# Layer A of a two-layer decoder: the compressed branch's softmax over two query blocks at once

## The chip, the cores and the metric

The kernel runs on one core of a Trainium2 chip. The metric is the device time of one execution in microseconds (us). Each kernel is timed several times and the median is quoted; one further execution is profiled, and its trace gives every row shown here.

## The reference, cut to what matters

A sequence of 512 tokens of width 1024 goes through two layers. Layer A's mixer is a sparse attention with three branches, joined by sigmoid gates, for 12 query heads of width 64 in 3 groups of 4 that share keys and values. The branch that the change touches is the first one:

```python
k_c = rope(rmsnorm(compress(split_heads(k_cmp, G), 0), k_norm[0]), cmp_end)   # 31 blocks of 32 tokens
v_c = compress(split_heads(v_cmp, G), 1)
m_c = cmp_end[None, :] <= t[:, None]
p_c = masked_softmax(jnp.einsum('bgrqd,bgcd->bgrqc', q_b, k_c) * scale, m_c)
o_c = jnp.einsum('bgrqc,bgcd->bgrqd', p_c.astype(v_c.dtype), v_c)
o_c = jnp.where(m_c.any(-1)[:, None], o_c, 0)
...
return g_b[..., 0:1] * o_c + g_b[..., 1:2] * o_s + g_b[..., 2:3] * o_w
```

So every query of every head has a softmax over at most 31 compressed keys, and the first 31 queries, which see none of them, get zero. The other two branches attend to all earlier tokens (with 512 tokens the selection and the window leave nothing out). Beside the mixer runs a small attention over 256 memory tokens; then come an output projection and an MLP, and layer B with a dilated attention, its own memory attention and its MLP.

## The kernel before, in words

**Tiles.** The 512 queries are 4 blocks of 128 (`NB = 4`). The large products are taken as three products of rounded halves (`mm3`, L241 to L247). Weights come by `wdma` (L213 to L216) on SyncE's queue into one of 3 `st` buffers, are split on ScalarE and VectorE (`wsplit`, L235 to L239, the instructions at L237 and L239) and are then free to be overwritten by the next load. Scores of attention go into the PSUM pool `pS` of 3 banks, turned probabilities into `pT` of 2 banks.

**Items and filler.** `attend` (L129) writes layer A's attention as a list of items. An item has a front (scores and softmax) and a back (transposes, and at some items the product with the values), and an item's back is written after the next item's front. After each front and each back a number of filler steps is written, `RA[group]` on average: steps of the projection of the next group (`proj_a`), of the memory keys and values (`mem_kv`), of the memory queries and of the output projection, in the order in which `layer_a` adds them to `work`. The third group's projection and the memory queries wait until all items of group 0 or 1 have had their front (`seen.count(0) == 20`, `seen.count(1) == 20`). The numbers 20 are 16 attention items and 4 compressed ones.

**Order on the engines.** What is written is not yet the order of the engines: the framework (`schedule_with_timeline_sim=True`, L1809) plans each engine's own order beforehand by its planned times. On the chip each engine then keeps to that order.

**The compressed branch.** `compress` (L822) makes the compressed keys `KC` and values `vc`; `vc` is written by a VectorE addition at L905. For each group `cmp_scores` (L935) makes `VCB`, in which the group's 32 compressed values stand four times on different partitions and columns: one clear on GpSimd (L941) and four copies of 32x64 on ScalarE (L943). An item (`front`, L948, and `back`, L973) is one block of 128 queries with the 4 heads of the group:

- 4 matmuls of 64 columns into one `pS` tile (L951);
- on VectorE two additions that read that tile (L956, L957), a maximum (L959), a subtraction (L960), after the exponential on ScalarE (L961) a sum (L963), a reciprocal (L964) and the gate's product (L969; L967 for the first block, with the factor that clears the first 31 queries);
- on GpSimd the product with gate over sum (L970), on TensorE one transpose (L975), and a copy out of PSUM by `evT`.

The tile on which this happens is `s_cs`, from a pool of **two** buffers (`cs=2`, L184): it is taken by L956 and is free again when the transpose L975 has read it. The `pS` bank is free when L957 has read it. `cmp_out` (L980) multiplies `VCB` with the transposed probabilities (L981) at the end of each pair of heads.

`evT` (L678) copies on VectorE (L682) where a running count of all tiles made, `self.n`, can be divided by 3, else on ScalarE (L684). So which engine copies depends on how many tiles have been made before.

Each group has 16 attention items (fronts at L1018 to L1022 for the first two blocks, at L1031 to L1034 for the others, exponentials at L1040, scaling on GpSimd at L676, transposes at L1061 and L1067, product with the values at L1080) and 4 compressed ones. `spread` sets these in after six attention items in group 0 and after one in groups 1 and 2, and from there every second item.

Of the kernel before, what the change touches and what calls it, by code (L numbers as in the profile page):

```python
# [10 lines left out]
BF16 = mybir.dt.bfloat16  # L11
# [36 lines left out]
RA = (1.5, 1.16, 1.46, 1.96)  # L48
# [119 lines left out]
class K:  # L168
# [193 lines left out]
    def setup(self):  # L362
        nc, ins = self.nc, self.ins
        on = self.c("on1", [P, P])
        nc.vector.memset(on, 1.0)
        self.on1 = on[:, 0:1]
        n = self.n
# [47 lines left out]
    def setup2(self):  # L415

        nc = self.nc
        self.x = [None] * KT
        self.idr = self.c("idr", [P, P], F32R)
        nc.vector.tensor_copy(self.idr, self.idf)  # L420
        self.idb, self.cm = [self.c(n, [P, P], BF16) for n in ("idb", "cm")]
        nc.vector.tensor_copy(self.idb, self.idf)
        nc.vector.tensor_copy(self.cm, self.cm0)
        for a, z, g in ((0, NQ, -(HD**-0.5) / KN), (NQ, NK, -1.0 / KN)):
            nc.vector.tensor_scalar(
                out=self.gr[:, a:z], in0=self.gr[:, a:z], scalar1=g, scalar2=None, op0=ALU.mult
            )
# [289 lines left out]
    def layer_a(self):  # L717
# [35 lines left out]
        work.add(self.proj_a(2, xg, st, ga[2]), "g2", lambda: seen.count(0) == 20)  # L753
        work.add(self.mem_q(0, xg, ins["w_am"], e, qm), None, lambda: seen.count(1) == 20)
# [5 lines left out]
        items = spread(L[0], C[0], 6, 1) + spread(L[1], C[1], 1, 1) + spread(L[2], C[2], 1, 1) + M  # L760
# [174 lines left out]
    def cmp_scores(self, g, q4, cmp, gt):  # L935
# [6 lines left out]
        for q in range(4):  # L942
            nc.scalar.activation(  # L943
                VCB[32 * q : 32 * q + 32, q // 2, (q % 2) * HD : (q % 2 + 1) * HD], vc[32 * g : 32 * g + 32, :], AF.Copy
            )
        pcT = self.t("x", [P, S])

        def front(i):  # L948
            Sc = self.ps(self.pS, [P, 4, 2, 32])
            for h in range(4):  # L950
                nc.tensor.matmul(  # L951
                    Sc[:, h].rearrange("p t c -> p (t c)"), q4[h // 2][:, h % 2, i * P : (i + 1) * P],
                    KC[:, g].rearrange("p t c -> p (t c)"), start=True, stop=True,
                )
            s = self.t("cs", [P, 4, 32])
            nc.vector.tensor_tensor(out=s, in0=Sc[:, :, 0], in1=bcast(self.ccm[:, i, :], 1, 4), op=ALU.add)  # L956
            nc.vector.tensor_tensor(out=s, in0=Sc[:, :, 1], in1=s, op=ALU.add)  # L957
            m = self.t("c1", [P, 4])
            nc.vector.tensor_reduce(out=m, in_=s, axis=AX.X, op=ALU.max)  # L959
            nc.vector.tensor_tensor(out=s, in0=s, in1=bcast(m, 2, 32), op=ALU.subtract)  # L960
            nc.scalar.activation(s, s, AF.Exp)  # L961
            z = self.t("c2", [P, 4])
            nc.vector.tensor_reduce(out=z, in_=s, axis=AX.X, op=ALU.add)  # L963
            nc.vector.reciprocal(out=z, in_=z)  # L964
            gc = gt[:, i, :].rearrange("p (h b) -> p h b", b=3)[:, 4 * g : 4 * g + 4, 0]
            if i == 0:
# [19 lines left out]
    def attn_a(self, g, ga, gt, cmp, out):  # L986
# [61 lines left out]
        def back(pr, half, hp, ii, p):  # L1048
# [43 lines left out]
            [Item(cfront, cback, (i,), g, "cmp") for i in range(NB)],  # L1092
# [721 lines left out]
```

## Time and profile before

| | us |
|---|---|
| median of 3 runs | 1267.33 |
| lowest and highest run | 1264.51, 1268.48 |
| the profiled execution, its own time | 1264.88 |
| its span from the first to the last instruction | 1263.1 |

TensorE's granted clock was 0.999 of full speed over the span. A row of the trace names the line, the engine (PE is TensorE's matmul, PEld its weight load, DVE VectorE, ACT ScalarE, POOL GpSimd, SPq SyncE's queue), the operation, the tile written and the tiles read, and the shapes. Idle time is put down to what ended it, the releaser. The attention of layer A lies between 97 and 300 us of the span; the last of the 12 compressed items ends at 244 us.

### The profile page before, as it was taken

The page shows a single profiled execution, that of the slowest core. Times are in us where ns is not written, and L with a number is a line of the kernel's source. Part 1 is how long each engine was busy: PE and PEld are TensorE (multiplying, and loading weights), DVE is VectorE, ACT ScalarE, POOL GpSimd, SP SyncE. Part 2 cuts the span into 40 slices and gives each one's busy share as a digit, 9 for nine tenths or more (in the row PEclk, how much of TensorE's full clock was granted, in tenths as well). Part 3 has the DMA queues.
Part 4 walks back from the last instruction along what each step waited for, and adds up shares of the span by engine and source line. Part 5 has one row for each costly group of instructions (what it writes and reads, how often), then busy time and mean ns, then how long its engine had stood idle before and what let it go on. Part 6 is the DMA issues. An engine that isn't in the chain of part 4 may idle for free.

```text
span 1263.1 us, 18587 instructions
## 1 busy us (share of the span) xinstructions
PE 1232.9 (98%) x6445; PEld 1013.6 (80%) x6445; DVE 971.0 (77%) x1793; ACT 762.9 (60%) x1763; POOL 416.2 (33%) x449
## 2 busy tenths in 40 slices
PE   9998999999999999999999999999999999999998
PEld 8776677677788888888888899888688888888887
DVE  6968878864679678686799968886678868678687
ACT  6656767774476464553656567887776455455462
POOL 0666465543133133250332612222313225033231
PEclk9999999999999999999999999999999999999999
DMA  8311311023532525326235332212242532624423
GB/s 312 112 63 62 108 35 60 9 68 105 162 101 84 167 84 173 120 92 184 99 104 173 108 117 59 68 35 80 86 141 83 172 117 96 183 99 140 142 85 117
DMA packets 52717, 139.10 MB, mean 110 GB/s; under 512 B 5680, under 2 KB 14896, under 8 KB 52624
## 3 DMA queue, kind: packets, MB, share of 16 engines
q1 hardware_dynamic: 51568, 135.50, 34.1%
q0 software_dynamic: 480, 1.38, 0.3%
q8 instruction: 51, 0.84, 0.3%
q10 hardware_dynamic: 576, 1.05, 0.2%
q14 instruction: 42, 0.34, 0.1%
HBM read 132.66 MB, written 5.24 MB: 109 GB/s over the span
## 4 chain that ended last, share of the span: by engine, by line
PE 87%; DVE 6%; ACT 3%; DMA 2%; issue 1%; POOL 1%; SPq 0%; POOLq 0%; DVEq 0%; ACTq 0%
PE s_ps L247 27%; PE s_ps L244 14%; PE s_acc L247 13%; PE s_pt L247 8%; PE s_acc L244 7%; PE s_pt L244 4%; PE s_po L1080 2%; PE s_acc L845 1%; PE s_ps L1031 1%; PE s_pt L1067 1%; PE s_ps L1541 1%; PE s_pt L701 1%; DVE s_w L263 1%; ACT s_w L237 1%; DMA s_st<-in_w_ag_dram 1%
## 5 line engine op out<-in xcount | busy, mean ns | idle before, releaser
L247 PE MATMUL s_ps<-s_act,s_w 128*128 128x512 f32 x1184 | 366.1, 390 | 0.0
L239 DVE TENSOR_TENSOR s_w<-s_st,s_w 128x1024 fp32r<-128x1024 f32 (+4 forms) x161 | 189.1, 1177 | 133.6 <-ACT s_w L237 133.4
L247 PEld LDWEIGHTS s_ps<-s_act,s_w 128*128 128x128 f32 x1184 | 221.7, 188 | 45.7 <-DVE s_act L285 0.4
L237 ACT ACTIVATE s_w<-s_st 128x1024 fp32r<-128x1024 f32 (+4 forms) x182 | 165.7, 918 | 143.2 <-PE s_pt L247 44.5
L244 PE MATMUL s_ps<-s_act,s_w 128*128 128x512 f32 x592 | 231.4, 393 | 3.1 <-DVE s_x L817 1.7
L247 PE MATMUL s_acc<-s_w,s_act 128*128 128x512 f32 (+2 forms) x608 | 169.5, 359 | 0.5 <-DVE s_w L263 0.5
L244 PEld LDWEIGHTS s_ps<-s_act,s_w 128*128 128x128 f32 x592 | 110.9, 188 | 28.4 <-ACT s_act L282 3.2
L247 PEld LDWEIGHTS s_acc<-s_w,s_act 128*128 128x128 f32 x608 | 109.1, 191 | 11.2 <-DVE s_w L263 0.7
L1131 POOL TENSOR_TENSOR s_x<-s_qki,s_st 128x512 f32<-128x512 f32 x16 | 25.3, 1582 | 270.8 <-DMA s_st<-in_w_db_dram 204.9
L244 PE MATMUL s_acc<-s_w,s_act 128*128 128x512 f32 (+2 forms) x304 | 111.2, 371 | 3.4 <-ACT s_w L237 3.4
L1131 POOL TENSOR_TENSOR s_x<-s_x,s_st 128x512 f32<-128x512 f32 x32 | 73.9, 2337 | 102.7 <-DVE s_w L239 102.7
L676 POOL TENSOR_SCALAR s_p<-s_p,s_cr 128x256 f32<-128x256 f32 (+3 forms) x128 | 69.3, 555 | 72.3 <-DVE s_cr L1043 35.2
L247 PE MATMUL s_pt<-s_w,s_act 128*128 128x512 f32 x288 | 86.7, 390 | 0.0
L237 ACT ACTIVATE s_w<-s_x 128x512 fp32r<-128x512 f32 x96 | 56.9, 625 | 48.4 <-POOL s_x L1131 32.2
L239 DVE TENSOR_TENSOR s_w<-s_x,s_w 128x512 fp32r<-128x512 f32 x96 | 68.8, 737 | 10.8 <-ACT s_w L237 10.7
L247 PE MATMUL s_ps<-s_w,s_qk 128*128 128x512 f32 x256 | 76.5, 389 | 0.0
L247 PE MATMUL s_acc<-s_w,s_qk 128*128 128x512 f32 x256 | 76.3, 390 | 0.0
L282 ACT ACTIVATE s_qk<-s_p 128x256 fp32r<-128x256 f32 (+1 forms) x96 | 46.9, 489 | 47.2 <-DVE s_p L1259 44.9
L285 DVE TENSOR_TENSOR s_qk<-s_p,s_qk 128x256 fp32r<-128x256 f32 (+1 forms) x96 | 71.8, 758 | 1.5 <-ACT s_qk L282 0.2
L244 PEld LDWEIGHTS s_acc<-s_w,s_act 128*128 128x128 f32 x304 | 57.8, 191 | 9.1 <-ACT s_w L237 3.9
L1253 ACT ACTIVATE s_p<-s_ps 128x512 f32<-128x512 f32 x64 | 37.8, 590 | 44.5 <-PE s_ps L247 43.9
L247 PEld LDWEIGHTS s_pt<-s_w,s_act 128*128 128x128 f32 x288 | 53.9, 188 | 11.2
(335 smaller groups left out, 2728.1 us busy)
## 6 DMA issues: line engine op xcount, KB each, us to landing
s_st<-in_w_db_dram SPq DMA_DIRECT2D x80, 512.0 KB, 3.6
s_st<-in_w_up_dram SPq DMA_DIRECT2D x64, 512.0 KB, 3.7
s_st<-in_w_bq_dram SPq DMA_DIRECT2D x16, 384.0 KB, 3.2
s_st<-in_w_ag_dram SPq DMA_DIRECT2D x11, 512.0 KB, 4.2
s_act<-in_w_c_dram SPq DMA_DIRECT2D x8, 512.0 KB, 5.7
s_st<-in_w_mem_dram SPq DMA_DIRECT2D x8, 512.0 KB, 3.5
s_st<-in_w_ao_dram SPq DMA_DIRECT2D x16, 256.0 KB, 2.8
s_tq<-in_w_db_dram SPq DMA_DIRECT2D x16, 256.0 KB, 3.0
```

The source lines that it names most:

```text
L237: self.high = nc.scalar.activation(w[:, 0], st, AF.Copy)
L239: self.low = e.tensor_tensor(out=w[:, 1], in0=st, in1=w[:, 0], op=ALU.subtract)
L244: mm(ps, lh[0], rh[0], start=start, stop=False, skip_group_check=again)
L247: self.last = mm(ps, lh[i], rh[j], start=False, stop=stop and i != wr, skip_group_check=again)
L263: nc.vector.scalar_tensor_tensor(out=dst[:, 1], in0=src, scalar=g, in1=dst[:, 0], op0=ALU.mult, op1=ALU.subtract),
L282: nc.scalar.activation(dst[:, 0], src, AF.Copy)
L285: nc.vector.tensor_tensor(out=dst[:, 1], in0=src, in1=dst[:, 0], op=ALU.subtract)
L676: self.nc.gpsimd.tensor_scalar(out=p, in0=p, scalar1=c, scalar2=1.0, op0=ALU.mult, op1=ALU.mult)
L701: nc.tensor.transpose(pt[:, h, :].bitcast(F32R), kpair(qi[:, j + h]), self.idr)
L1080: nc.tensor.matmul(O[x * 64 : x * 64 + 64, q0 + o : q0 + 256], v[:, j, br, :], st[x][br][:, j, o:256], start=half == 0 and br == 1 and j = ...
L1131: (e or self.nc.gpsimd).tensor_tensor(out=o, in0=x, in1=b[:, i * 512 : (i + 1) * 512], op=ALU.add)
L1253: nc.scalar.activation(u, ps, AF.Relu)
```

## The change

1. A compressed item takes **two** query blocks: 8 score matmuls into one tile of 512 columns, one chain of VectorE operations of 256 elements (an extra small one for the first pair of a group, in place of the fused gate product), one exponential, one GpSimd product, two transposes into one tile and one copy. There are 2 items in a group, 6 in all, for 4 and 12.
2. `VCB` is filled by four transfers on SyncE's queue for each group, not by four ScalarE copies.
3. The items stand further apart: in group 0 after six attention items and again after four more, in groups 1 and 2 after one and again after three more. The counts 20 become 18, and group 2's share of filler rises from 1.46 to 1.65 steps.
4. The `cs` buffers grow from 512 to 1024 bytes per partition. To make room, the matrix of ones for TensorE's first, idle matmuls lives in a `cs` buffer at the start, only one column of ones is kept, and the 16-bit identity is written over the first half of the mask that has just been copied.

```diff
-RA = (1.5, 1.16, 1.46, 1.96)
+RA = (1.5, 1.16, 1.65, 1.96)
...
-        on = self.c("on1", [P, P])
+        n = self.n
+        self.on1 = self.c("on1", [P, 1])
+        on = self.t("cs", [P, P])
         nc.vector.memset(on, 1.0)
-        self.on1 = on[:, 0:1]
-        n = self.n
+        nc.vector.memset(self.on1, 1.0)
...
-        self.idb, self.cm = [self.c(n, [P, P], BF16) for n in ("idb", "cm")]
+        self.cm = self.c("cm", [P, P], BF16)
+        nc.vector.tensor_copy(self.cm, self.cm0)
+        self.idb = self.cm0[:, 0 : P // 2].bitcast(BF16)
         nc.vector.tensor_copy(self.idb, self.idf)
-        nc.vector.tensor_copy(self.cm, self.cm0)
...
-        work.add(self.proj_a(2, xg, st, ga[2]), "g2", lambda: seen.count(0) == 20)
-        work.add(self.mem_q(0, xg, ins["w_am"], e, qm), None, lambda: seen.count(1) == 20)
+        work.add(self.proj_a(2, xg, st, ga[2]), "g2", lambda: seen.count(0) == 18)
+        work.add(self.mem_q(0, xg, ins["w_am"], e, qm), None, lambda: seen.count(1) == 18)
...
-        items = spread(L[0], C[0], 6, 1) + spread(L[1], C[1], 1, 1) + spread(L[2], C[2], 1, 1) + M
+        items = spread(L[0], C[0], 6, 4) + spread(L[1], C[1], 1, 3) + spread(L[2], C[2], 1, 3) + M
...
         for q in range(4):
-            nc.scalar.activation(
-                VCB[32 * q : 32 * q + 32, q // 2, (q % 2) * HD : (q % 2 + 1) * HD], vc[32 * g : 32 * g + 32, :], AF.Copy
+            nc.sync.dma_start(
+                VCB[32 * q : 32 * q + 32, q // 2, (q % 2) * HD : (q % 2 + 1) * HD], vc[32 * g : 32 * g + 32, :]
             )
...
-            Sc = self.ps(self.pS, [P, 4, 2, 32])
-            for h in range(4):
+            Sc = self.ps(self.pS, [P, 2, 4, 2, 32])
+            two = slice(2 * i, 2 * i + 2)
+            for j in range(2):
+                for h in range(4):
...
-            s = self.t("cs", [P, 4, 32])
-            nc.vector.tensor_tensor(out=s, in0=Sc[:, :, 0], in1=bcast(self.ccm[:, i, :], 1, 4), op=ALU.add)
-            nc.vector.tensor_tensor(out=s, in0=Sc[:, :, 1], in1=s, op=ALU.add)
+            s = self.t("cs", [P, 2, 4, 32])
+            nc.vector.tensor_tensor(out=s, in0=Sc[:, :, :, 0], in1=bcast(self.ccm[:, two, :], 2, 4), op=ALU.add)
+            nc.vector.tensor_tensor(out=s, in0=Sc[:, :, :, 1], in1=s, op=ALU.add)
...
+            nc.vector.tensor_tensor(out=z, in0=z, in1=gc, op=ALU.mult)
             if i == 0:
-                nc.vector.scalar_tensor_tensor(out=z, in0=z, scalar=self.zc, in1=gc, op0=ALU.mult, op1=ALU.mult)
-            else:
-                nc.vector.tensor_tensor(out=z, in0=z, in1=gc, op=ALU.mult)
+                nc.vector.tensor_scalar(out=z[:, 0], in0=z[:, 0], scalar1=self.zc, scalar2=None, op0=ALU.mult)
...
-            pt = self.ps(self.pT, [P, P])
-            nc.tensor.transpose(pt, s.rearrange("p h c -> p (h c)"), self.idf)
-            self.evT(pcT[:, i * P : (i + 1) * P], pt)
+            pt = self.ps(self.pT, [P, 2, P])
+            for j in range(2):
+                nc.tensor.transpose(pt[:, j], s[:, j].rearrange("p h c -> p (h c)"), self.idf)
+            self.evT(pcT[:, 2 * i * P : 2 * i * P + 2 * P].rearrange("p (j q) -> p j q", j=2), pt)
...
-            [Item(cfront, cback, (i,), g, "cmp") for i in range(NB)],
+            [Item(cfront, cback, (i,), g, "cmp") for i in range(NB // 2)],
```

## Rows read from the trace of the kernel before

**Rows 1.** The page's first part: busy time of each engine, share of the span and number of instructions.

```profile
PE 1232.9 (98%) x6445; PEld 1013.6 (80%) x6445; DVE 971.0 (77%) x1793; ACT 762.9 (60%) x1763; POOL 416.2 (33%) x449
```

**Rows 2.** Busy time by stretch: the stretch, its length, the busy time and instructions of each engine, the granted clock, the DMA share and GB/s.

```profile
97.00:151.00 54.00, 46.12 (x296) 34.97 (x295) 46.24 (x123) 41.81 (x123) 30.72 (x40) 1.00 0.30 99
151.00:205.00 54.00, 54.00 (x353) 44.22 (x351) 41.62 (x112) 34.49 (x112) 35.44 (x51) 1.00 0.14 40
205.00:258.00 53.00, 48.47 (x356) 33.39 (x355) 41.25 (x120) 38.89 (x122) 25.50 (x45) 1.00 0.08 26
```

**Rows 3.** What TensorE waited for from 97 to 151 us: the waiting matmul, the releaser, us in total, times, the longest.

```profile
PE s_acc L244 <- ACT s_w L237: 2.8, 2, 1.9
PE s_ps L1018 <- ACT s_p L1040: 1.5, 1, 1.5
PE s_ps L951 <- DVE s_cs L957: 1.2, 1, 1.2
...
PE s_ps L1031 <- DVE s_cs L957: 0.6, 1, 0.6
```

**Rows 4.** The same from 205 to 258 us.

```profile
PE s_ps L1031 <- ACT s_p L1040: 1.0, 4, 0.5
...
PE s_ps L1031 <- DVE s_cs L957: 0.3, 1, 0.3
PE s_ps L951 <- ACT s_p L1040: 0.3, 1, 0.3
```

**Rows 5.** The chain of work that ended last, from 108 to 134 us: start, us, what. Six more pieces of L943 lie at the first "...", so the eight copies fill 114.50 to 116.47 us.

```profile
114.50 0.11 ACT s_ki L943
...
116.22 0.25 ACT s_ki L943
...
116.50 1.06 ACT s_w L237
...
117.58 1.24 DVE s_w L239
...
118.84 3.37 DMA s_st<-in_w_mem_dram
...
123.99 4.03 DMA s_st<-in_w_ag_dram
```

**Rows 6.** TensorE in order of time (start, us, what): scores of the third and fourth compressed item of group 0 and the transpose of its first; scores of the third item of group 2 and the transpose of its first.

```profile
110.73 0.61 PE L951 MATMUL s_ps<-KC,s_qk 128*128 128x64 f32 x4
...
115.08 0.61 PE L951 MATMUL s_ps<-KC,s_qk 128*128 128x64 f32 x4
...
121.87 0.27 PE L975 MATMUL s_pt<-c,s_cs 128*128 128x128 f32 x1
...
225.49 0.63 PE L951 MATMUL s_ps<-KC,s_qk 128*128 128x64 f32 x4 [0.28 <-ACT s_p L1040]
...
231.86 0.27 PE L975 MATMUL s_pt<-c,s_cs 128*128 128x128 f32 x1
```

**Rows 7.** VectorE in order of time, in brackets the idle time before and its releaser.

```profile
113.25 0.21 DVE L905 TENSOR_TENSOR s_ab<-s_pt,gr 96x64 f32<-96x64 f32 x1
...
124.47 0.28 DVE L957 TENSOR_TENSOR s_cs<-s_ps,s_cs 128x128 f32<-128x128 f32 x1
...
130.88 0.28 DVE L957 TENSOR_TENSOR s_cs<-s_ps,s_cs 128x128 f32<-128x128 f32 x1
...
148.61 0.28 DVE L956 TENSOR_TENSOR s_cs<-s_ps,c 128x128 f32<-128x128 f32 x1
148.81 0.21 DVE L506 SCALAR_TENSOR_TENSOR s_r<-s_r,ec,s_r 128x4 f32<-128x4 f32 x1
...
200.72 0.41 DVE L574 TENSOR_TENSOR s_tq<-s_acc,gr 128x256 f32<-128x256 f32 x1
201.05 0.15 DVE L507 SCALAR_TENSOR_TENSOR s_r<-s_r,s_r 128x4 f32<-128x4 f32 x1
201.12 0.15 DVE L1042 RECIPROCAL s_cr<-s_su 128x2 f32<-128x2 f32 x1
...
232.17 0.29 DVE L956 TENSOR_TENSOR s_cs<-s_ps,c 128x128 f32<-128x128 f32 x1 [2.17 <-PE s_pt L975]
```

**Rows 8.** Groups of instructions by line and shape, 0 to 400 us: busy us, mean ns of one, the idle time before them and its releasers.

```profile
L943 ACT ACTIVATE s_ki<-s_ab 32x64 f32<-32x64 f32 x12 | 3.0, 253 | 0.1
...
L961 ACT ACTIVATE s_cs<-s_cs 128x128 f32<-128x128 f32 x12 | 3.8, 315 | 3.5 <-DVE s_cs L960 3.1 <-DVE s_c L969 0.3
...
L970 POOL TENSOR_TENSOR s_cs<-s_cs,s_c 128x128 f32<-128x128 f32 x12 | 4.8, 397 | 5.9 <-DVE s_c L969 4.9 <-DVE s_cr L1042 0.8 <-PE s_pt L1067 0.2
...
L682 DVE COPY s_pt<-s_pt 128x384 f32<-128x384 f32 x10 | 5.5, 551 | 3.6 <-PE s_pt L1067 3.6
...
L682 DVE COPY s_pt<-s_pt 128x256 f32<-128x256 f32 x6 | 2.5, 419 | 3.1 <-PE s_pt L1061 2.3 <-PE s_po L1080 0.5
...
L682 DVE COPY s_x<-s_pt 128x128 f32<-128x128 f32 x3 | 0.8, 282 | 2.3 <-PE s_pt L975 2.3
```

**Rows 9.** SyncE's queue in order of time (a row of two issues spans both), and the first use of `VCB` on TensorE (a group's row: shortest, median and longest ns, first and last start).

```profile
102.33 9.44 SPq L215 DMA_DIRECT2D s_st<-in_w_mem_dram  x2
...
118.84 0.33 SPq L215 DMA_DIRECT2D s_st<-in_w_mem_dram  x1
...
L981 PE MATMUL s_po<-s_x,s_ki x10: 592/594/697, 141.0 to 255.9; 128*128 128x512 f32 x10
```

More of the change, by code (lines that the diff above doesn't have):

```diff
@@ L948, in front @@
         def front(i):
-            Sc = self.ps(self.pS, [P, 4, 2, 32])
-            for h in range(4):
[L951 to L954, printed above, removed]
-            s = self.t("cs", [P, 4, 32])
-            nc.vector.tensor_tensor(out=s, in0=Sc[:, :, 0], in1=bcast(self.ccm[:, i, :], 1, 4), op=ALU.add)
-            nc.vector.tensor_tensor(out=s, in0=Sc[:, :, 1], in1=s, op=ALU.add)
@@ L958, in front @@
-            m = self.t("c1", [P, 4])
+            Sc = self.ps(self.pS, [P, 2, 4, 2, 32])
+            two = slice(2 * i, 2 * i + 2)
+            for j in range(2):
+                for h in range(4):
+                    nc.tensor.matmul(
+                        Sc[:, j, h].rearrange("p t c -> p (t c)"),
+                        q4[h // 2][:, h % 2, (2 * i + j) * P : (2 * i + j + 1) * P],
+                        KC[:, g].rearrange("p t c -> p (t c)"), start=True, stop=True,
+                    )
@@ L959, in front @@
+            s = self.t("cs", [P, 2, 4, 32])
+            nc.vector.tensor_tensor(out=s, in0=Sc[:, :, :, 0], in1=bcast(self.ccm[:, two, :], 2, 4), op=ALU.add)
+            nc.vector.tensor_tensor(out=s, in0=Sc[:, :, :, 1], in1=s, op=ALU.add)
+            m = self.t("c1", [P, 2, 4])
             nc.vector.tensor_reduce(out=m, in_=s, axis=AX.X, op=ALU.max)
-            nc.vector.tensor_tensor(out=s, in0=s, in1=bcast(m, 2, 32), op=ALU.subtract)
+            nc.vector.tensor_tensor(out=s, in0=s, in1=bcast(m, 3, 32), op=ALU.subtract)
@@ L961, in front @@
             nc.scalar.activation(s, s, AF.Exp)
-            z = self.t("c2", [P, 4])
+            z = self.t("c2", [P, 2, 4])
             nc.vector.tensor_reduce(out=z, in_=s, axis=AX.X, op=ALU.add)
             nc.vector.reciprocal(out=z, in_=z)
-            gc = gt[:, i, :].rearrange("p (h b) -> p h b", b=3)[:, 4 * g : 4 * g + 4, 0]
+            gc = gt[:, two, :].rearrange("p i (h b) -> p i h b", b=3)[:, :, 4 * g : 4 * g + 4, 0]
+            nc.vector.tensor_tensor(out=z, in0=z, in1=gc, op=ALU.mult)
@@ L966, in front @@
             if i == 0:
-                nc.vector.scalar_tensor_tensor(out=z, in0=z, scalar=self.zc, in1=gc, op0=ALU.mult, op1=ALU.mult)
-            else:
-                nc.vector.tensor_tensor(out=z, in0=z, in1=gc, op=ALU.mult)
-            nc.gpsimd.tensor_tensor(out=s, in0=s, in1=bcast(z, 2, 32), op=ALU.mult)
+                nc.vector.tensor_scalar(out=z[:, 0], in0=z[:, 0], scalar1=self.zc, scalar2=None, op0=ALU.mult)
+            nc.gpsimd.tensor_tensor(out=s, in0=s, in1=bcast(z, 3, 32), op=ALU.mult)
@@ L998, in cback @@
             cs[3](i, s)
-            if i == NB - 1:
+            if i == NB // 2 - 1:
                 cs.append(True)
```

## The prediction

> **What bounds the kernel now.** I read the page first: TensorE is busy 98% of the span, VectorE 77%, ScalarE 60% [rows 1]. That looks like a kernel which only TensorE's own work can shorten. The table of busy time by stretch says where this holds. From 151 to 205 us TensorE is busy all 54.00 us: what other engines save there is worth nothing. From 97 to 151 it is busy 46.12 of 54 and from 205 to 258 48.47 of 53, while VectorE has 46.24 (86%) and 41.25 (78%) [rows 2]. In these two stretches, 12.4 us of idle TensorE together, attention runs with little filler, and there I asked what TensorE waited for. Three kinds matter. Late weights: 2.8 us for the split of L237. Score banks: matmuls of L951, L1018 and L1031 need one of the three `pS` banks, and wait for L957 or L1040 to free it: 3.3 us in the first stretch [rows 3], 1.6 in the second [rows 4]. The rest are copies out of `pT`, which the change hardly touches.
>
> Two things behind these waits belong to the compressed branch. First, the chain of waits goes through the eight `VCB` copies of groups 0 and 1 on ScalarE: 114.50 to 116.47 us, and right behind them the weight split at 116.50, VectorE's part at 117.58, which frees the `st` buffer for the load at 118.84 [rows 5]. TensorE's longest wait for L237, 1.9 us [rows 3], ends there. Second, the two `s_cs` buffers. The third item's scores of group 0 are in their bank from 110.73, but L956 can't start before the first item's transpose at 121.87 [rows 6]; the bank is free after L957 at 124.47, some 14 us later. The fourth item's goes from 115.08 to 130.88 [rows 6, 7]. From 115 to 124 two of three banks are shut in. In group 2 the third item's scores start at 225.49, and VectorE, which keeps its order, stands 2.17 us until the transpose at 231.86 [rows 6, 7].
>
> **The change, part by part.** TensorE's work stays: 48 matmuls and 12 transposes, so no term.
>
> *Transfers for copies.* Twelve copies of 253 ns leave ScalarE, 3.0 us [rows 8]; eight of them stood in the chain. With them away the split starts up to 2.0 us earlier, and TensorE's 1.9 us wait behind it can go. Bounds: nothing (the split then waits for something else), and all 2.8 us. I take 1.9, by the row of that wait. The transfers cost SyncE 12 issues of 0.33 us [rows 9]. Eight of them, 2.6 us, can go out once `vc` is written at 113.46 (113.25 and 0.21) [rows 7], until 116.1, and the queue's next load, at 118.84 before, would be wanted at about 116.8: just room. The third group's four come later, where the queue idles. `VCB` is first read at 141.0 [rows 9], over 20 us later; a transfer of 512 KB lands in 3.37 us [rows 5], so one of 8 KB costs no wait unless that cover goes, when it would cost up to those 3.4 us. GpSimd clears `VCB` as before; a late clear would now hold SyncE's queue. For groups 0 and 1 it is done before the copies begin at 114.50 [rows 5].
>
> *Pairs for single items: the banks.* A group now takes two `s_cs` buffers and has two, and pairs lie four or five items apart, so no pair waits for the transpose of another of its group. The banks no longer stay shut for 14 us. The pair fills a whole bank and holds it longer by four matmuls (about 0.45 us, from 0.61 for four that overlap [rows 6]) and two wider additions (0.13 us each, below). Of the 4.9 us of bank waits [rows 3, 4]: L1018's 1.5 ends when ScalarE gets to L1040, which itself stands behind splits, so half of it, 0.7; L951's and L1031's 1.8 behind L957 come from the first two items, which become one, so one of two remains, the larger: 0.6 gained; of the second stretch's 1.6, in which the shut banks lie, half: 0.8. Together 2.1; bounds 0 and 4.9. Late next is the weight split or ScalarE's copies out of `pT`.
>
> *Pairs: VectorE's time.* An operation of 128 elements keeps the engine 0.20 us (148.61 to 148.81), one of 256 0.33 (200.72 to 201.05), a small one 0.07 (201.05 to 201.12) [rows 7]. A pair so saves 5 times 0.07 and 2 times 0.07, about 0.5 us, six pairs 3.0, less 0.2 for three new small operations: 2.8 for 39 operations fewer. Fewer tiles also move `evT`'s count. I stepped it through the written order: it gives the 38 VectorE copies that the trace has, and 32 after; four of 384 elements, two of 256 and three of 128 leave VectorE and three of 256 come. At their durations less the 0.08 that the next one overlaps (0.47, 0.34, 0.20 [rows 8]) that is 2.2 us more, so 5.0 in all, 3.6 of it in the two stretches. About 0.3 of TensorE's wait there ends on VectorE (2.1 of the 7.7 us in the rows [rows 3, 4]): 1.0 us. Bounds 0 and 3.6.
>
> *VectorE's fixed cost, by a second measure.* The Trainium skill ("VectorE: DVE Perf Modes", section "The TRN2 errata — SBUF-src ops pay a fixed extra latency per instruction") gives a measured fixed term of about 150 cycles of a 0.96 GHz clock for each instruction. By it 39 operations fewer would be worth an estimated 6.1 us of VectorE, and this term about 1.6 us instead of 1.0. The trace does not agree: 0.20 against 0.33 us leaves 0.07 us fixed in back-to-back use [rows 7].
>
> *ScalarE and GpSimd.* Twelve exponentials of 315 ns become six of at most twice that: nothing or a gain. Six more attention copies come to ScalarE (four of 384, two of 256, about 3 us by VectorE's rows), against 3.0 us of `VCB` copies that went: even. Twelve GpSimd products of 397 ns become six, at most as long in sum [rows 8]. All off the path; each would cost at most what it adds.
>
> *Spacing and filler.* Stepping the loop, written filler runs out for 3 ticks in group 0 where it was 7, for 1 in group 1 where it was 5, and in group 2 it ends at the same items. The engines' own order is planned anyway: I count nothing, between a loss of one more 1.9 us wait and a gain of as much. The smaller constants at the start (one more clear, two copies swapped) cost under 0.3 us.
>
> **Sum:** 1.9 + 2.1 + 1.0 = 5.0 us. The profiled execution took 1264.88 us, so 1259.9 by its own time; the median of the runs is 2.45 higher, so **1262.3**. A measurement of this kernel tells no change from a change under 0.3%, 3.8 us.
>
> **Rivals.**
> *The weights set group 0's stretch.* Behind the load at 118.84 (3.37 us) comes one at 123.99 (4.03 us) on the same chain [rows 5], and freed banks and VectorE time only make TensorE reach the next weight sooner. For it: the longest wait is for L237. Against: the waits for banks lie in the same stretch. Then 1.9 remains, of the banks only the second stretch's 0.8, of VectorE's half: 3.2 in all, 1264.1. Chance 0.22.
> *The transfers sit in the wrong place of the queue,* ahead of the load that was issued at 111.44 (the end of the two-issue row, less 0.33) [rows 9]. SyncE would wait for `vc` until 113.46 and issue eight: the load leaves at 116.1, lands 3.4 us later at 119.5, and the split moves from 116.50 to there, 3.0 us later instead of 1.9 sooner. 5.0 less 4.9: 1267.2. For it: the plan is made before the run and the queue can't swap. Against: the load is ready 2 us earlier. Chance 0.12.
> *The pair stands in the way of the attention items* (slower). It takes one whole bank of three through eight matmuls and two wide additions that queue on VectorE; the next attention score waits at TensorE. If each of the six pairs costs the 1.5 us of L1018's wait, 8.8 us, and the bank gain is gone, 2.9 remain against it: 5.9 slower, 1273.2. From about 1.1 us a pair on it is slower by more than 3.8. For it: L957 already freed its bank late, three times in the two stretches. Against: twelve holds of a bank become six, and none lasts 14 us. Chance 0.14.
>
> **Chances.** The forecast keeps 0.52. Of it 0.45 lies beyond 3.8 us, as do 0.05 of the weights' rival: faster 0.50. Slower is 0.13 of the pair's rival and 0.01 of the queue's: 0.14. The rest, 0.36, is the same. The range goes from all upper bounds, 2.8 + 4.9 + 3.6 = 11.3, that is 1256.0, up to 1269.5, where half of the slower rival's case and more of the queue's lie within.
>
> **What would show it.** Right: no ScalarE work on `s_ki`; the split behind 116 us earlier by near 2 us; L951 to L957 within 5 us at all six pairs, none ended by L975; waits for `pS` in the two stretches under 3 us; VectorE's copies in layer A 32. TensorE busy all of the middle stretch as before, and layer B as long as before. Wrong: SyncE standing before a transfer into `s_ki` while a weight is wanted; new waits of L1018 or L1031 for L957; or the same waits a little later, for L237.

## The result, and the profile after

The kernel after takes 1260.11 us (median of 5 runs, 1259.43 to 1261.05) against 1266.71 us before (5 runs beside them): the ratio is 0.9948, 95% interval [0.9932, 0.9963], so 6.6 us less (4.7 to 8.6). Forecast were 5.0 us less and a range of 1256.0 to 1269.5.

The profiled execution of after took 1261.05 us, the longest of its five, that of before 1264.88, shorter than four of its five, so their spans differ by only 3.8 us (1263.1 and 1259.3). The lines of the changed functions stand two to five further down: L951 is now L955, L957 is L962, L975 is L980, L943 is L945, L1031 is L1036, L1061 and L1067 are L1066 and L1072, `evT`'s L682 and L684 are L684 and L686.

The busy times and instruction counts of the page, against [rows 1]:

```profile
PE 1235.2 (98%) x6445; PEld 1014.8 (81%) x6445; DVE 959.6 (76%) x1749; ACT 761.0 (60%) x1745; POOL 415.5 (33%) x443
```

TensorE has the same 6445 matmuls, VectorE 44 instructions and 11.4 us less, GpSimd 6 fewer. Busy time by stretch, with the columns of [rows 2]:

```profile
97.00:151.00 54.00, 48.86 (x286) 36.49 (x285) 44.76 (x109) 38.62 (x109) 30.67 (x37) 0.94 0.31 100
151.00:205.00 54.00, 54.00 (x363) 44.55 (x362) 39.12 (x99) 34.54 (x106) 36.49 (x51) 1.00 0.13 41
205.00:258.00 53.00, 49.65 (x363) 33.84 (x361) 37.05 (x106) 41.59 (x129) 25.45 (x44) 1.00 0.08 26
```

The middle stretch is full, as before. The first has 2.74 us less idle TensorE than in [rows 2], the third 1.18. In the first the granted clock is 0.94; a part of its busy time is matmuls at the lower clock (last section), and fewer of them begin in it, 286 for 296: in these two executions the first stretch gained nothing by its end. What TensorE still waited for from 97 to 151 us:

```profile
PE s_acc L244 <- ACT s_w L237: 1.2, 1, 1.2
PE s_pt L1072 <- DVE s_pt L684: 1.1, 1, 1.1
...
PE s_ps L1036 <- ACT s_p L1045: 0.4, 1, 0.4
```

Of the waits for `pS` banks, 3.3 us in [rows 3], 0.4 is left, and the split L237 stands for 1.2 us instead of 2.8. From 205 to 258 us, where [rows 4] have 1.6 us of bank waits:

```profile
PE s_pt L1066 <- ACT s_qk L661: 1.1, 1, 1.1
...
PE s_ps L1036 <- ACT s_p L1045: 0.3, 1, 0.3
```

The first and the second pair of group 0 on TensorE, then VectorE (start, us, what), for [rows 6, 7]:

```profile
101.76 0.97 PE L955 MATMUL s_ps<-KC,s_qk 128*128 128x64 f32 x8
...
106.18 0.41 DVE L962 TENSOR_TENSOR s_cs<-s_ps,s_cs 128x256 f32<-128x256 f32 x1
...
113.49 1.06 PE L955 MATMUL s_ps<-KC,s_qk 128*128 128x64 f32 x8
...
117.56 0.42 DVE L962 TENSOR_TENSOR s_cs<-s_ps,s_cs 128x256 f32<-128x256 f32 x1
```

A pair holds its bank 4.8 and 4.5 us; the other four pairs hold theirs for about 2 to 3 us. Nothing like the 14 us of the third single item is left. SyncE's queue, for [rows 9], and the group of the new transfers (shortest, median, longest ns of the issue):

```profile
112.95 3.15 SPq L945 DMA_DIRECT2D s_ki<-s_ab  x5
116.22 0.52 SPq L215 DMA_DIRECT2D s_st<-in_w_mem_dram  x1
116.78 1.77 SPq L945 DMA_DIRECT2D s_ki<-s_ab  x3
122.59 7.79 SPq L215 DMA_DIRECT2D s_st<-in_w_ag_dram  x4
```

```profile
L945 SPq DMA_DIRECT2D s_ki<-s_ab x12: 507/582/625, 113.0 to 174.6; - x12
```

The load that left at 118.84 us in [rows 5] leaves at 116.22, behind five of the transfers. The chain shows it with the split ahead of it:

```profile
113.07 1.03 ACT s_w L237
...
114.12 1.43 DVE s_w L239
...
116.22 4.01 DMA s_st<-in_w_mem_dram
...
120.25 1.06 ACT s_w L237
...
122.59 3.38 DMA s_st<-in_w_ag_dram
```

The split that was at 116.50 is at 113.07, 3.4 us earlier; the next one, 120.25, follows the load that now takes 4.01 us to land. Whether the transfers did this, the run e_copies below tells.

**Where along the kernel the time goes** is read best from the start of the n-th matmul, since all kernels here have 6445. How much later than in the kernel after each starts it (us; the head row is that kernel's own time), worked out from the single profiled executions of all kernels, those of the next section among them. Where the orders differ the n-th matmul can be another one, so what counts is a difference that lasts. The last column has where, up to 358 us, the granted clock fell to 0.50, for 3.4 us unless a length is given in brackets:

```
start in after      103   123   144   176   204   218   247   264   279   315   358   clock down from
matmul              500   600   700   900  1100  1200  1400  1500  1600  1800  2000
after                                                                                 137.9 (6.8)
before              0.8   4.4  -0.1  -0.2   0.4   1.8   2.1   2.1   3.7   3.6   3.6   -
e_setup             0.9   7.1   3.4   3.1   3.7   5.0   5.3   5.3   6.9   6.8   6.8   117.7, 128.0
e_transfers         0.8   2.2  -0.9  -1.0  -0.3   0.9   1.2   1.2   2.8   2.7   2.7   -
e_four              0.6   2.6   0.1  -0.1   0.5   2.0   0.1   0.1   1.7   1.6   1.5   131.6
e_four_transfers    0.6   1.6  -1.1  -1.2   0.2   1.6  -0.3  -0.3   2.9   2.8   2.8   130.2, 273.6
e_copies            0.5   1.6   0.7  -0.4   0.5   0.8   0.8   0.8   0.7   0.7   0.7   130.4, 140.6
e_one               0.3   0.7   0.5  -0.6   0.4   0.7   3.0   2.7   2.6   2.5   2.5   130.9, 141.2, 243.6
e_close             1.9  11.4   8.5   8.3   9.7  10.0  11.3  11.3  11.4  11.4  11.4   103.3 (30.7)
e_close_first       0.9   7.3   4.4   4.1   4.8   5.1   5.1   5.1   5.0   5.0   5.0   104.5 (6.8), 118.2 (6.8)
e_close_late        0.5   0.4  -0.6  -0.4   0.8   0.7   1.9   1.9   2.0   2.0   2.0   138.1
e_ra                0.5   0.1   0.6   1.0   1.0   0.8   0.9   0.5   3.5   9.4   8.2   129.1, 139.4 (6.8), 275.9
e_ra_middle         0.5  -0.1   0.5   0.9   1.3   1.1   1.0   1.5   2.2   2.4   1.7   129.2, 139.4 (6.8)
e_share             0.9   6.6   6.4   6.1   6.9   8.4   9.6   9.8  10.8  11.1  10.6   119.0, 136.1 (6.8)
```

Before is 4.4 us behind at 123 us; after has lost that lead by 144 us and wins 3.3 us from 204 to 279 us. Its clock, down for 6.8 us from 137.9, is a part of that loss and not all: e_transfers, whose clock stays up, also gives back 1.4 of the 2.2 us that it leads before by at 123 us. Before's profile has no such dip in layer A, so it flatters the kernel before. The profile of e_setup, which is timed like before, has the mean clock of after's, 0.995; it is 3.4 us behind at 144 us, 3.7 at 204 and 6.9 at 279. So at like clock the gain has two halves, group 0's stretch and group 2's. Before is 3.6 us behind at 358 us and 3.8 at the end: the change acts in layer A's attention alone, and layer B is as long as before.

### The profile page after: what moved, and what is told of

It reads as the page before. It is cut to its first block, busy times and chain, and to the rows that moved or that the text cites. A ratio compares the mean times of both kernels' runs of the same rounds, so it can differ in the third digit from the quotient of the medians.

```text
span 1259.3 us, 18527 instructions
## 1 busy us (share of the span) xinstructions
PE 1235.2 (98%) x6445; PEld 1014.8 (81%) x6445; DVE 959.6 (76%) x1749; ACT 761.0 (60%) x1745; POOL 415.5 (33%) x443
## 4 chain that ended last, share of the span: by engine, by line
PE 86%; DVE 6%; ACT 4%; DMA 2%; POOL 1%; issue 1%; SPq 0%; POOLq 0%; DVEq 0%; ACTq 0%
PE s_ps L247 27%; PE s_ps L244 14%; PE s_acc L247 13%; PE s_pt L247 8%; PE s_acc L244 7%; PE s_pt L244 4%; PE s_po L1085 1%; PE s_acc L847 1%; PE s_ps L1036 1%; PE s_ps L1546 1%; DVE s_w L239 1%; DMA s_st<-in_w_ag_dram 1%; PE s_pt L703 1%; PE s_pt L1072 1%; ACT s_p L1045 1%
## 5 line engine op out<-in xcount | busy, mean ns | idle before, releaser
L247 PE MATMUL s_ps<-s_act,s_w 128*128 128x512 f32 x1184 | 366.0, 391 | 0.0
L247 PEld LDWEIGHTS s_ps<-s_act,s_w 128*128 128x128 f32 x1184 | 221.5, 188 | 45.7 <-DVE s_act L285 0.4
L237 ACT ACTIVATE s_w<-s_st 128x1024 fp32r<-128x1024 f32 (+4 forms) x182 | 165.7, 918 | 148.9 <-PE s_pt L247 44.5
L244 PE MATMUL s_ps<-s_act,s_w 128*128 128x512 f32 x592 | 231.3, 393 | 3.1 <-DVE s_x L819 1.7
L247 PE MATMUL s_acc<-s_w,s_act 128*128 128x512 f32 (+2 forms) x608 | 171.2, 360 | 0.8 <-DVE s_w L263 0.5
L244 PEld LDWEIGHTS s_ps<-s_act,s_w 128*128 128x128 f32 x592 | 110.9, 188 | 28.4 <-ACT s_act L282 3.2
L247 PEld LDWEIGHTS s_acc<-s_w,s_act 128*128 128x128 f32 x608 | 109.5, 191 | 11.4 <-DVE s_w L263 0.7
L244 PE MATMUL s_acc<-s_w,s_act 128*128 128x512 f32 (+2 forms) x304 | 111.3, 371 | 2.1 <-ACT s_w L237 1.2
L1136 POOL TENSOR_TENSOR s_x<-s_qki,s_st 128x512 f32<-128x512 f32 x16 | 22.7, 1417 | 271.6 <-DMA s_st<-in_w_db_dram 211.4
L247 PE MATMUL s_pt<-s_w,s_act 128*128 128x512 f32 x288 | 86.7, 390 | 0.0
L237 ACT ACTIVATE s_w<-s_x 128x512 fp32r<-128x512 f32 x96 | 56.9, 625 | 48.6 <-POOL s_x L1136 33.0
L247 PE MATMUL s_ps<-s_w,s_qk 128*128 128x512 f32 x256 | 76.5, 389 | 0.0
L247 PE MATMUL s_acc<-s_w,s_qk 128*128 128x512 f32 x256 | 76.3, 390 | 0.0
L244 PEld LDWEIGHTS s_acc<-s_w,s_act 128*128 128x128 f32 x304 | 57.9, 192 | 7.4 <-ACT s_w L237 1.7
L247 PEld LDWEIGHTS s_pt<-s_w,s_act 128*128 128x128 f32 x288 | 53.9, 188 | 11.2
```

Source lines behind the costliest of these rows:

```text
L237: self.high = nc.scalar.activation(w[:, 0], st, AF.Copy)
L244: mm(ps, lh[0], rh[0], start=start, stop=False, skip_group_check=again)
L247: self.last = mm(ps, lh[i], rh[j], start=False, stop=stop and i != wr, skip_group_check=again)
L1136: (e or self.nc.gpsimd).tensor_tensor(out=o, in0=x, in1=b[:, i * 512 : (i + 1) * 512], op=ALU.add)
```

## The experiments

Each ran in five rounds beside the kernel before (medians of 1266.46 to 1266.77 us, 23 to 32 runs); ratios are to it, and a difference in us is that of two ratios times 1266.6. **The theory** was that of the prediction: ScalarE's copies ahead of the split, `s_cs` buffers that shut banks, and VectorE's time add up; spacing and filler share do nothing. **The rivals**: one of the parts alone carries the gain, or the new order of the work does. A ratio's interval is about 1.5 us to a side, and executions of one kernel differ by their mean granted clock (last section), so differences of 1 to 2 us are read together with the table and the clock.

### Smaller constants alone (e_setup)

```diff
-        on = self.c("on1", [P, P])
+        self.on1 = self.c("on1", [P, 1])
+        on = self.t("cs", [P, P])
...
+        self.idb = self.cm0[:, 0 : P // 2].bitcast(BF16)
```

> The kernel before with only the smaller constants of the change (ones in a cs buffer, the 16-bit identity over the mask). The change's trace ran 0.4 us ahead of before's at the first attention item already. If these constants do it: 0.4 us faster, ratio 0.9997, within noise of none. Rival: they move buffers and so the planned order, and a part of the 6.6 us is theirs: 1 to 2 us faster. The theory of waits gives 0 to 0.4.

Measured: 1266.69 us, 0.9994 [0.9983, 1.0005]. No gain or loss clear of noise; the interval does not exclude the rival's 1 to 2 us.

### Transfers alone (e_transfers)

The kernel before with `VCB` by `nc.sync.dma_start`:

```diff
-            nc.scalar.activation(VCB[...], vc[32 * g : 32 * g + 32, :], AF.Copy)
+            nc.sync.dma_start(VCB[...], vc[32 * g : 32 * g + 32, :])
```

> The kernel before, with its 12 single items, and only VCB filled by transfers. Theory of the chain: the weight split no longer stands behind eight copies on ScalarE (2.0 us of the chain), TensorE's 1.9 us wait goes: 1.5 to 2.0 us faster, ratio about 0.9986. Rival (the copies were covered, the pairs do it all): 0. Rival (queue): transfers ahead of a weight load, up to 3 us slower.

Measured: 1264.69 us, 0.998 [0.9968, 0.9991], 2.5 us less. TensorE's waits from 97 to 151 us, for [rows 3]:

```profile
PE s_ps L951 <- DVE s_cs L957: 1.2, 1, 1.2
...
PE s_ps L1031 <- ACT s_p L1040: 0.9, 1, 0.9
PE s_ps L1018 <- DVE s_cs L957: 0.8, 1, 0.8
...
PE s_ps L1031 <- DVE s_cs L957: 0.6, 1, 0.6
PE s_acc L244 <- ACT s_w L237: 0.3, 1, 0.3
```

The wait for the split fell from 2.8 to 0.3 us, the bank waits stayed (3.5 us for 3.3). So the first term's mechanism is shown in the kernel before. The split's start is at 114.9 us for 116.50. Its size is less sure. Idle TensorE in this stretch fell by 1.3 us only (7.9 to 6.6), and in the table this kernel leads before by 0.9 us at 358 us, not 2.5. The rest of the 2.5 seems to go with the granted clock: 6 of these 12 runs have a mean clock of 0.999 or 1.0, of the 23 of the kernel before beside them 4. At 0.999 the medians are 1264.30 (3 runs) and 1265.33 (4): 1.0 us. Whether the shorter wait keeps the clock up, or these runs met fewer dips for another reason, is not shown.

### Four buffers alone (e_four)

The kernel before with the smaller constants and `cs=4`: twelve single items, ScalarE's copies.

```diff
-        cs=2, stt=4, ab=1,
+        cs=4, stt=4, ab=1,
```

> The kernel before with the smaller constants and four s_cs buffers for two: still 12 single items, ScalarE copies, close spacing. No third item then waits for the first one's transpose. If the shut banks are what the pairs cure: L951 to L957 under 5 us at all items and 2 us faster (0.6 to 3). Rival (the saving is VectorE's time and the wider spacing): holds shrink and the time stays within 0.5 us of the constants-only kernel.

Measured: 1263.48 us, 0.9968 [0.9955, 0.9981], 4.1 us less. VectorE's additions for the third and fourth item of group 0, for those at 124.47 and 130.88 in [rows 7] (here L959):

```profile
113.48 0.25 DVE L959 TENSOR_TENSOR s_cs<-s_ps,s_cs 128x128 f32<-128x128 f32 x1
...
116.65 0.29 DVE L959 TENSOR_TENSOR s_cs<-s_ps,s_cs 128x128 f32<-128x128 f32 x1
```

They come 11 and 14 us earlier; the banks are held 3 and 2 us. In group 2 the holds of the third and fourth item fall from 7.3 and 9.8 us to 2.3 and 2.2. So opening the banks brings 4.1 us, about twice the 2.1 that I took, and a pair isn't needed for it: a buffer for every item does the same. At a mean clock of 0.997 it is 3.2 us (1263.46, 4 runs, for the 1266.66 of the kernel before). What TensorE waited for from 97 to 151 us is instructive:

```profile
PE s_ps L1033 <- ACT s_p L1042: 2.2, 3, 1.4
PE s_ps L953 <- DVE s_cs L959: 1.2, 1, 1.2
PE s_acc L244 <- ACT s_w L237: 1.0, 2, 0.7
...
PE s_ps L1033 <- DVE s_cs L959: 0.6, 1, 0.6
```

The waits that name a bank have not fallen, 4.0 us for 3.3 in [rows 3]. The split's has, from 2.8 to 1.0. The split itself starts at 115.78 us, behind six of the eight copies, for 116.50 behind all of them; that the open banks brought other work forward, and the split with it, is my reading and not shown. From 205 to 258 us the bank waits fell, from 1.6 us in [rows 4] to 0.7, and the table has about 2 us of the gain between 218 and 247 us.

### Four buffers and transfers (e_four_transfers)

The edits of the last two together, still twelve single items.

> The kernel before with the smaller constants, four s_cs buffers and VCB by transfers: everything of the change but the pairing, its spacing and its filler share. The four buffers alone measured 0.9968, the transfers alone 0.9980. If they add up: 0.9948, as the whole change, and the pairing is worth nothing beside the buffers that it frees. If VectorE's saved time counts as predicted (1.0 us): 0.9956. Rival (the pairing is worth most): not better than 0.9968.

Measured: 1262.73 us, 0.9966 [0.9954, 0.9978], 4.3 us less, not 6.6. That looks as if the two did not add up, and both do shorten the wait for the split L237; but each of the three gains is uncertain by about 1.5 us, and at equal clock they add up: 1.0 (at 0.999) and 3.2 (at 0.997) for 3.8 (at 0.997, 1262.83, 3 runs). It is 2.3 us short of the change. The two intervals do not quite part them, but at a mean clock of 0.997 the runs do: 1262.73 to 1262.95 (3) against 1259.43 to 1260.11 (4), 2.8 us. The table's 2.8 us from the 1600th matmul on agrees by size, though about half of it is a dip of the clock at 273.6 us. So 2.3 to 2.8 us of the gain are left to the pairs with their spacing and filler share.

### The change with ScalarE's copies (e_copies)

The diff of e_transfers backwards, on the kernel after.

> The changed kernel with VCB again filled by ScalarE copies. Theory: the eight copies come back into the chain and 1.9 of the 6.6 us are lost: about 4.7 us faster than before, ratio 0.9963. Rival (pairs do it all): 6.6 us faster, 0.9948. Rival (the transfers cost a later weight load): more than 6.6 us faster.

Measured: 1261.45 us, 0.9955 [0.9941, 0.9969]. 0.9 us of the 6.6 go, and the table has 0.7: within the uncertainty neither nothing nor the theory's 1.9 is excluded. But the mechanism is not the theory's. ScalarE in order of time, in this kernel with its copies:

```profile
113.57 1.06 ACT L237 ACTIVATE s_w<-s_st 128x1024 fp32r<-128x1024 f32 x1
114.54 2.10 ACT L945 ACTIVATE s_ki<-s_ab 32x64 f32<-32x64 f32 x8
```

The split stands ahead of the eight copies, at 113.57 us; in the kernel after it is at 113.07. So of the 3.4 us by which the change brings it forward, 2.9 come without the transfers, from the new order of the work.

### The change with one buffer (e_one)

```diff
-        cs=2, stt=4, ab=1,
+        cs=1, stt=4, ab=1,
```

> The changed kernel with a single s_cs buffer: the second pair of a group can't start before the first pair's transposes. Theory of the buffers: the second pair's scores shut a bank in again, in group 0 for 5 us or more where it was 4.3, in group 2 more than 2.8; of the 6.6 us 1 to 2 are lost, 0.9960. Rival (pairs stand so far apart that a buffer is always free): the same 0.9948.

Measured: 1262.49 us, 0.9968 [0.9955, 0.998]: 2.5 us lost, with an uncertainty of nearly as much. In group 2 the second pair waits for the first one's transpose again:

```profile
224.84 1.08 PE L955 MATMUL s_ps<-KC,s_qk 128*128 128x64 f32 x8
...
234.52 0.38 PE L980 MATMUL s_pt<-c,s_cs 128*128 128x128 f32 x2
...
236.64 0.41 DVE L962 TENSOR_TENSOR s_cs<-s_ps,s_cs 128x256 f32<-128x256 f32 x1
```

A bank is held for 12 us, and the table shows the loss there: 0.7 us behind at 218 us, 3.0 at 247 us, a part of it a dip of the clock from 243.6 us. In group 0 the second pair held its bank for 9.2 us (113.8 to 123.1), as expected, but there the table shows no loss: what a shut bank costs depends on what else TensorE can do at the time.

### The change with close pairs (e_close)

```diff
-        items = spread(L[0], C[0], 6, 4) + spread(L[1], C[1], 1, 3) + spread(L[2], C[2], 1, 3) + M
+        items = spread(L[0], C[0], 6, 1) + spread(L[1], C[1], 1, 1) + spread(L[2], C[2], 1, 1) + M
```

> The changed kernel with its two pairs of a group as close as the single items were (one attention item between them). Theory: two pairs still have two buffers, so no bank is shut in: within 1 us of the change, 0.9941 to 0.9956. Rival (the spacing does it): 2 us or more are lost, 0.9964 or worse.

Measured: 1270.49 us, 1.0024 [1.0011, 1.0038]: 9.6 us over the change, and slower than before. The theory fell here. TensorE in order of time:

```profile
99.96 0.62 PE L247 MATMUL s_acc<-s_w,s_act 128*128 128x512 f32 x2
102.89 0.35 PE L875 MATMUL s_pt<-c,s_raw 96*128 96x96 f32 x2 [2.31 <-DVE s_raw L870]
103.03 1.23 PE L955 MATMUL s_ps<-KC,s_qk 128*128 128x64 f32 x6
```

The transpose L875 of `compress`'s values waits 2.31 us for VectorE's L870. In the kernel after the planner had put matmuls of the projection (L244, L247) there, and L875 behind the first pair:

```profile
101.08 0.39 PE L244 MATMUL s_acc<-s_w,s_act 128*128 128x512 f32 x1
101.31 0.62 PE L247 MATMUL s_acc<-s_w,s_act 128*128 128x512 f32 x2
101.76 0.97 PE L955 MATMUL s_ps<-KC,s_qk 128*128 128x64 f32 x8
...
104.98 0.33 PE L875 MATMUL s_pt<-c,s_raw 96*128 96x96 f32 x2
```

No line of `compress` or of the first pair was changed; only where the second pair is written. And the idle time has a sequel. The stretches of e_close, columns as in [rows 2]:

```profile
97.00:103.00 6.00, 3.69 (x18) 2.72 (x17) 5.97 (x11) 3.38 (x10) 5.13 (x6) 1.00 0.20 57
103.00:134.00 31.00, 26.02 (x112) 18.57 (x113) 20.13 (x54) 20.14 (x56) 17.62 (x24) 0.50 0.21 62
```

From 103 to 134 us the granted clock is 0.50, that is 1.2 GHz, behind a stretch in which TensorE was idle 2.31 of 6 us. In the kernel after:

```profile
97.00:103.00 6.00, 6.00 (x32) 5.00 (x31) 5.96 (x10) 3.72 (x11) 4.63 (x4) 1.00 0.02 7
103.00:134.00 31.00, 27.36 (x174) 20.50 (x173) 25.18 (x59) 22.10 (x58) 21.03 (x26) 1.00 0.37 122
```

174 matmuls begin there in 31 us, against 112. By the table 9.5 of the 11.4 us are lost between the 500th and the 600th matmul. It is no chance of one execution: the mean clock of all 11 runs is 0.986 to 0.992.

### Close in group 0 alone, and in groups 1 and 2 alone (e_close_first, e_close_late)

```diff
-spread(L[0], C[0], 6, 4) + spread(L[1], C[1], 1, 3) + spread(L[2], C[2], 1, 3)
+spread(L[0], C[0], 6, 1) + spread(L[1], C[1], 1, 3) + spread(L[2], C[2], 1, 3)   # first
+spread(L[0], C[0], 6, 4) + spread(L[1], C[1], 1, 1) + spread(L[2], C[2], 1, 1)   # late
```

> The change with group 0's two pairs close (one attention item between them instead of four), groups 1 and 2 spaced as in the change. Close spacing everywhere gave 9.6 us over the change, with TensorE at the 1.2 GHz level for 30.7 us right behind group 0's first pair. Theory P (the two pairs of group 0, eight wide additions and sixteen matmuls in a row with little filler, make TensorE idle there, and the clock follows): this run loses most of the 9.6 us, ratio to the kernel before 1.000 to 1.004, with a long half-clock stretch from about 103 us. Rival Q (the later groups' spacing costs): within 2 us of the change, ratio about 0.995.

Measured: 1268.41 us, 1.0022 [1.0012, 1.0032]: nearly all of the loss. The same idle time, and the lower clock behind it, for 6.8 us from 104.5 us, and again for 6.8 from 118.2, in the profiled execution, which is one of the shorter of its 12. The first of the two:

```profile
97.00:103.00 6.00, 3.69 (x18) 2.72 (x17) 5.96 (x11) 3.40 (x10) 5.13 (x6) 1.00 0.18 49
...
104.50:111.30 6.80, 6.80 (x32) 5.38 (x31) 6.74 (x16) 3.33 (x9) 5.28 (x6) 0.50 0.27 79
```

> The change with the pairs of groups 1 and 2 close (one attention item between them instead of three), group 0 spaced as in the change. Theory P (group 0 sets the loss): within 2 us of the change, ratio about 0.995 to 0.996. Rival Q (the later groups' spacing sets it): ratio 1.000 to 1.004, and the layer's markers level with the change until about 150 us, late after it.

Measured: 1263.69 us, 0.9978 [0.9968, 0.9988]: 3.8 us over the change, more than theory P allowed and less than rival Q. Group 0's order makes most of the loss (P), but the later groups are not free: the table has this kernel 0.4 us ahead at 176 us and 1.9 behind at 247. The expectation that the loss sits in one place was wrong.

### Group 2's filler share (e_ra, e_ra_middle, e_share)

```diff
-RA = (1.5, 1.16, 1.65, 1.96)
+RA = (1.5, 1.16, 1.46, 1.96)   # e_ra: the change with the old share
+RA = (1.5, 1.16, 1.58, 1.96)   # e_ra_middle: the change, in between
```

> The changed kernel with group 2's filler share back at 1.46. I counted the retuning at nothing: within 1 us of the change, 0.9941 to 0.9956. Rival: with four ticks fewer the filler of group 2 no longer ends with its items, the output projection starts late, and 2 us or more are lost.

Measured: 1268.32 us, 1.0009 [0.9998, 1.0021]: 7.7 us over the change, another miss. Steps are written by items: group 2 has 18 items and 36 turns now, 52.6 steps at 1.46, where the memory queries, keys and values before the output projection take 56 by a count in the program. The kernel before had 20 items, 58.4 steps; the change's 1.65 gives 59.4. The table has e_ra level up to 264 us and 9.4 us behind at 315. The output projection's first addition (L1125 before) is at 295 us, in the kernel after at 279. The stretch 255 to 330 us in both, after first:

```profile
255.00:330.00 75.00, 73.82 (x407) 56.77 (x407) 42.97 (x92) 40.62 (x107) 23.07 (x32) 1.00 0.35 105
```

```profile
255.00:330.00 75.00, 70.63 (x377) 52.14 (x376) 33.30 (x77) 39.51 (x106) 22.78 (x31) 0.98 0.28 82
```

3.2 us more of idle TensorE, a dip of the clock behind it (from 275.9 us) and 30 matmuls fewer: the projection that should fill the memory attention comes late.

> The change with group 2's filler share at 1.58 instead of 1.65. Group 2 has 18 items, 36 turns, and so writes 56.9 filler steps where 56 stand before the output projection; 1.46 wrote 52.6 and lost 7.8 us, 1.65 writes 59.4, the kernel before 40 times 1.46, 58.4. Theory S (the share only has to cover the 56 steps): within 1.5 us of the change, ratio 0.994 to 0.996, output projection's first addition near 279 us in the profile. Rival T (each step later costs): in proportion, 2.9 us lost, ratio 0.997.

Measured: 1262.54 us, 0.9974 [0.9964, 0.9984]: 3.3 us lost. Theory S said at most 1.5, rival T 2.9: the medians go with T, about 1.1 to 1.3 us a step (3.3 us for 2.5 steps, 7.7 for 6.8). It is not settled: the difference is uncertain by some 2 us, the profile is 1.7 us behind at 358 us, half of it already at 176, ahead of group 2, and its first addition of the output projection is at 281.0 us, near 279 as S said.

> The kernel before with group 2's filler share at the change's 1.65 and nothing else: 40 turns write 66 steps where 58.4 stood. Theory S (the new share only makes good for the four turns that pairing takes out of group 2, and is worth nothing by itself): ratio 0.999 to 1.002. Rival U (the share itself brings a part of the 6.6 us, the 2 us that transfers and buffers leave): ratio 0.998 to 0.9985.

Measured: 1266.81 us, 1.0011 [0.9999, 1.0022]. The new share in the kernel before brings nothing: it makes good for the turns that pairing takes away. (Its row of the table is from an execution of 1270.85 us, next to the longest of the 12.)

## Why the prediction was right, and where it was not

**Right by sign and nearly by size:** 5.0 us against 6.6 (4.7 to 8.6). What it named as signs is there: L955 to L962 within 5 us at all six pairs, 0.7 us of `pS` waits in the two stretches, 32 copies, a full middle stretch. But its three terms are not what was measured, and that their sum came near is in part luck.

**Transfers, 1.9.** The mechanism held in the kernel before: by transfers alone the split went 1.6 us forward, TensorE's wait for it fell, and the time by 2.5 us, of which 1.0 is left at equal clock. In the change it is not what happened: there the split goes 3.4 us forward, and 2.9 with ScalarE's copies still in place (e_copies), since the new order puts it ahead of them. The issue was mis-sized: 0.58 us, not 0.33, so 7.0 us of SyncE for 12. "Just room" was right by luck of the order: five transfers stand ahead of the load and three behind it. All eight ahead would have held it until about 117.6 us, an estimate from 112.95 and eight issues.

**Banks, 2.1.** Right in mechanism, too small: 4.1 alone, 3.2 at equal clock. The error was the view: I took halves of the waits that name a bank [rows 3, 4]; with four buffers those did not fall in the first stretch, and the time came out of the split's wait and of group 2. My bounds, 0 and 4.9, hold it.

**VectorE, 1.0.** The 32 copies are as stepped: 19, 6, 4 and 3. With overlaps counted once, the compressed items keep VectorE busy for 14.4 us instead of 18.8 and `evT`'s copies for 17.3 instead of 20.0: 7.0 us less where I had 5.0. The other 4.3 of the 11.4 us lie in operations that the change does not touch. A wide addition of `s_cs` takes 415 ns, a narrow one 280 [rows 7]: twice the elements cost 135 ns more, which leaves about 145 fixed in one instruction. The Trainium skill's fixed term of about 150 cycles, 156 ns ("VectorE: DVE Perf Modes", section "The TRN2 errata — SBUF-src ops pay a fixed extra latency per instruction"), agrees with that duration. My 0.07 us was that of instructions that overlap: the additions and the reductions do (0.06 to 0.09 us, worked out in the same way), the subtraction L960 does not (0.20). What this freed time is worth by itself no run tells apart; it lies in the 2.3 to 2.8 us that buffers and transfers leave to the change, together with the spacing and the filler share.

**The step that failed** is "Spacing and filler": "The engines' own order is planned anyway: I count nothing, between a loss of one more 1.9 us wait and a gain of as much". The written order is the planner's input, and moves work that the diff doesn't touch: with close pairs 9.6 us are lost, with the old filler share 7.7, either one more than the whole gain. The sum came out since the change has both right. With either old value it would have read as slower or the same, and I would have looked for the cause in the pair.

**Sums.** By their medians 2.5 (transfers) and 4.1 (buffers) give 4.3 together; at equal clock 1.0 and 3.2 give 3.8. So that the terms fill the same idle time of TensorE, and must not be added, is not shown. Against 1.9, 2.1 and 1.0 stand, at equal clock and from few runs each, about 1.0 for the transfers, 3.2 for the buffers and 2.8 for the pairs with their spacing and share: the first term was too large, the other two too small, and a part of the errors cancelled.

**The rivals.** *Weights*: one wait of 1.2 us for the split is left, so they did not take over. *Place in the queue*: the load left 2.6 us earlier, not late. SyncE did stand 3.0 us before the first transfer, for `vc`, but no load was due then; the five transfers held the load from 115.55, when its buffer was split, to 116.22 us. *The pair stands in the way*: not for banks, since none of the new waits names L962. Still, a slower kernel lay close by, by another mechanism: an order in which TensorE has nothing to do ahead of the first pair, and the clock behind it.

**Left open.** Why the planner moves L875 ahead of the projection's matmuls when the second pair is written earlier is not shown; neither is what part of the last 2.3 to 2.8 us is VectorE's freed time and what part the new order, nor whether a share above 1.65, or four single-item buffers with a spacing of their own, would do better than the change. No kernel tried here beat it.

## What to carry to other kernels

When items become fewer and larger, count again everything that is dealt out by item: here the old filler share or close spacing costs more than the whole change brings. Don't price a buffer that holds up a chain by the waits that happen to name the resource behind it: they gave 2.1 us here for a measured 3.2 to 4.1. Before you call two gains additive or not, compare runs at equal mean clock. To find where two orders part, compare the start of the n-th matmul: it needs no line to match. And when an experiment puts one part back, look where its instructions now stand: the copies that had stood ahead of the split came back behind it.

## What the runs showed of the hardware

**The clock.** TensorE's granted clock falls to 0.50 (1.2 GHz), here for 3.4, 6.8 and once 30.7 us. Two cases beside those above, the kernel before, then the kernel after (columns as in [rows 2]):

```profile
825.00:830.60 5.60, 4.05 (x28) 3.05 (x26) 5.60 (x17) 4.51 (x15) 0.83 (x1) 1.00 0.43 117
830.60:834.00 3.40, 3.37 (x16) 3.28 (x17) 3.08 (x12) 3.03 (x11) 0.00 (x0) 0.51 0.37 112
```

```profile
130.00:137.90 7.90, 6.55 (x55) 4.71 (x51) 6.90 (x11) 7.19 (x19) 4.00 (x5) 1.00 0.74 248
137.90:144.70 6.80, 6.65 (x21) 4.00 (x20) 3.48 (x14) 4.88 (x15) 2.50 (x4) 0.50 0.35 122
```

In both TensorE had been idle for 1.4 to 1.6 us in the stretch ahead. But the same idle time is not always followed by a dip: TensorE's wait of 1.9 us for the split L237 ends near 117.6 us both in before and in e_setup, and only in e_setup's profile the clock falls, at 117.7. The mean clock differs between executions of one kernel, and with it the time: of the kernel before, 11 runs with a mean clock of 0.999 have a median of 1264.61 us, 14 with 0.997 1266.66. At 0.997 the kernel after has 1260.01 (4 runs), so at equal clock the change brings 6.7 us. Two profiles with unequal dips, as here, show less.

**Small transfers.** One of 32 x 64 elements (8 KB) from one on-chip buffer to another takes SyncE 0.58 us to issue and lands in 1.8 us (median; longest 3.9); a weight load of 512 KB on the same queue takes 0.33 to 0.52 us to issue.
